# First SwiGLU, last two down parts: the four sums of weight blocks made by accumulating transfers, in two more raw buffers

## The chip, the cores and the metric

The kernel runs on one core of a Trainium2 chip. The metric is the device time of one execution in microseconds (us). A core has TensorE (PE, matrix products), VectorE (DVE), ScalarE (ACT), GpSimd (POOL) and SyncE (SP), which run their own rows of instructions in order and wait for each other by semaphores. Transfers between HBM and the on-chip memory are issued by SP, ACT or POOL and carried out by 16 DMA engines that all issuers share. A transfer issued by POOL can add what it reads to what lies at its destination (an accumulating transfer).

## The reference

Two layers of a decoder, sequence 512, width 1024, all in float32. Each layer is SwiGLU, a mixer with two kinds of attention, and a second SwiGLU:

```python
D_MODEL, SEQ, DEPTH, D_FF = 1024, 512, 2, 2816

def _swiglu(h, w_gate_up, w_down):
    g, u = jnp.split(h @ w_gate_up, 2, axis=-1)
    return (jax.nn.silu(g) * u) @ w_down

for layer in range(DEPTH):
    x = x + 0.5 * _swiglu(_rmsnorm(x, ffn1_norm[layer]), ffn1_w_gate_up[layer], ffn1_w_down[layer])
    x = x + _hybrid_mixer(_rmsnorm(x, mix_norm[layer]), w_in[layer], ...)
    x = x + 0.5 * _swiglu(_rmsnorm(x, ffn2_norm[layer]), ffn2_w_gate_up[layer], ffn2_w_down[layer])
return _rmsnorm(x, final_norm)
```

The change touches `@ w_down` of the first SwiGLU of layer 0 alone.

## The kernel before

**Products.** Float32 precision comes from splitting each operand into a high and a low half (`split`: ScalarE casts the value to the high half, line 86, VectorE subtracts to get the low half, line 87) and taking three matmuls of the halves (`mm3`, lines 421 to 423). A large product is cut into 2 x 2 blocks and made by seven block products instead of eight (a Strassen-Winograd scheme). On the weight side these need four sums of the blocks 11, 12, 21, 22. The seven products are named by digits and run in the order `STEADY = "1562734"`. Their weight operands are: 1: block 11; 2: block 12; 4: block 22; 5: 21 + 22; 7: 11 + 21; 6: 11 + 21 + 22; 3: 12 + 11 + 21 + 22.

**Parts.** A SwiGLU's inner width 2816 is cut into six parts (counted from 0). For each part there is a gate-up stage ("u") and a down stage ("d"); the order is u0, u1, d0, u2, d1, ... u5, d4, d5. The next part's turned hidden block (`turn_h`: transposes on TensorE, copies on ScalarE, differences on VectorE, lines 523 to 530) is made while the down stage before it runs. Each product of a down stage is 12 matmuls, followed by two updates of x on VectorE (line 552).

**Weights.** `forms` makes the weight operand of each product, in order. `get` loads a block (or a sum) into a raw buffer, 128 x 1024 floats (512 KB): `raw_tile` issues plain loads on SP (line 104); the sums for 5 and 7 get the second block by an accumulating transfer that POOL issues (line 137). The sum for 6 is made on VectorE by adding 5's sum to block 11 in place (line 148), and that for 3 by adding this result to block 12 (line 152). `make` splits the raw operand into one of five ring tiles (`wg`). Raw buffers have fixed names: down parts 4 and 5 of the first SwiGLU use s2 (11), R2 (7), V0 (22), V3 (12) and s0 (5); the gate-up part u5 before them uses among others s1 and V2. A raw buffer is given to its next user when the products in `last` are made.

**Order.** The program is written in the order of the products, with each weight made four products ahead (`next_w(ahead=4)`) and loads asked for up to 6 or 9 products ahead (the first number of each unit). A scheduler then fixes the row of each engine, and waits are added between the rows. Rows run in order: what waits on an engine holds up all that stands behind it there.

Of the kernel before, what the change touches and what calls it, by code (L numbers as in the profile page):

```python
# [12 lines left out]
ALU = mybir.AluOpType  # L13
# [42 lines left out]
def trunk(ctx, tc, xT, x, gains, gain_row, w_gu, w_dn, w_in, w_ff, w_out, fbias, lams, subln, consts, rope, out):  # L56
    nc = tc.nc
    act, dve, pool, pe, sp = nc.scalar, nc.vector, nc.gpsimd, nc.tensor, nc.sync
# [16 lines left out]
    def home(tag, shape, dt, name):  # L75
        return sb.tile(shape, dt, tag=tag, name=name, bufs=1)
# [13 lines left out]
    def split_w(src, hi, lo):  # L90
        w = min(step[0], src.shape[-1])
        for o in range(0, src.shape[-1], w):
            split(src[:, o:o + w], hi[:, o:o + w], lo[:, o:o + w])
        return hi, lo

    def ring_tile(tag, cols):
        g = home(tag, [P, 2, 1024], F32R, "wg")
        return g[:, 0, :cols], g[:, 1, :cols]

    def raw_tile(tag, cols, src):  # L100
        t = home(tag, [P, 1024], F32, "raw")
        w = min(step[0], cols)
        for o in range(0, cols, w):
            sp.dma_start(out=t[:, o:o + w], in_=src[:, o:o + w])
        return t[:, :cols]
# [6 lines left out]

    busy = set()

    def forms(order, groups, cols, where):

        raw = {}
        keys = [(f, h) for f in order for h in range(groups)]
        if order == FIRST:

            keys[:2 * groups] = [(f, h) for h in range(groups) for f in order[:2]]
        seen = set()

        last = {"11": ("2", "6"), "12": ("3",), "22": ("4",), "5": ("5", "6"), "7": ("7",)}

        def get(b, h, must=True):
            if (b, h) in raw:
                return raw[b, h]
            tag = where(b, h)[0]
            if tag in busy:  # L130
                assert not must, (tag, b, h)
                return None
            busy.add(tag)
            if b in "57":
                one, two = {"5": ("21", "22"), "7": ("11", "21")}[b]
                t = raw_tile(tag, cols, where(one, h)[1])
                pool.dma_start(out=t, in_=where(two, h)[1], accum_op=ALU.add)  # L137
            else:
                t = raw_tile(tag, cols, where(b, h)[1])
            raw[b, h] = t  # L140
            return t
        uses = {"1": "11", "2": "12", "5": "5", "6": "5", "3": "12", "7": "7", "4": "22"}

        def make(f, h, tag):
            src = get(uses[f], h)
            if f == "6":
                src = get("11", h)
                dve.tensor_tensor(out=src, in0=get("5", h), in1=src, op=ALU.add)
            w = split_w(src, *ring_tile(tag, cols))
            seen.add((f, h))  # L150
            if f in "26" and ("2", h) in seen and ("6", h) in seen:
                dve.tensor_tensor(out=raw["12", h], in0=raw["12", h], in1=raw["11", h], op=ALU.add)
            for b, fs in last.items():
                if f in fs and all((g, h) in seen for g in fs):
                    busy.discard(where(b, h)[0])
            return w
        return [(9 if f in "57" else 6, lambda f=f, h=h: get(uses[f], h, False),
                 lambda tag, f=f, h=h: make(f, h, tag)) for f, h in keys]

    def push(units, i):  # L160
# [6 lines left out]
    def gu_units(n, c, order):  # L167
        groups = PARTS_OF[n][c] // 256
        base = sum(8 if w == 512 else 4 for w in PARTS_OF[n][:c])
        tags = {("11", 0): "R0", ("11", 1): "R1", ("7", 0): "R2", ("22", 0): "V0", ("7", 1): "V1",  # L170
                ("22", 1): "V2", ("12", 0): "V3", ("12", 1): "V4", ("5", 0): "s0", ("5", 1): "s1"}
        if groups == 1:

            tags = {(b, 0): tags[b, 1] for b in ("11", "7", "22", "12", "5")}
        return forms(order, groups, 1024, lambda b, h: (
            tags.get((b, h)), w_gu[n, base + BLOCKS.index(b) * groups + h] if b in BLOCKS else None))

    def dn_units(n, c, order, second=False):
        cols = PARTS_OF[n][c] // 256 * 512
        base = sum(PARTS_OF[n][:c]) // 256 * 4 * 512  # L180
        tags = {"11": "s2", "7": "R2", "22": "V0", "12": "V3", "5": "s0"}
        if second:

            tags = {"11": "R1", "7": "V1", "22": "V4", "12": "V2", "5": "s1"}
            if n % 2 == 0:
                tags.update({"7": "R0", "22": "R0"})

        def where(b, h):
            src = None
            if b in BLOCKS:  # L190
                o = base + BLOCKS.index(b) * cols
                src = w_dn[n, o * P:(o + cols) * P].rearrange("(p s) -> p s", p=P)
            return tags.get(b), src
        return forms(order, 1, cols, where)

    def plain(src, raw_tag, tag):
        got = []
# [15 lines left out]
    NCH = len(PARTS_OF[0])  # L213
# [12 lines left out]
    def pair_units(n):  # L226
        own = {s: iter(dn_units(n, NCH - 2 + i, "".join(u[0] for u in PAIR if u[1] == s), i == 1))
               for i, s in enumerate("ab")}
        return [next(own[u[1]]) for u in PAIR]
# [7 lines left out]
    for n in range(2 * DEPTH):  # L237
        l = n // 2
        if n % 2 == 1:
            for i in range(24 + len(OUT_K)):  # L240
                k = OUT_K[i - 24] if i >= 24 else None
                tag = MIX[i % 3] if i < 24 else None if k >= 4 else MIX[(i - 28) % 3]
                stream.append(plain(w_in[l, i] if i < 24 else w_out[l, k], f"R{(i + 1) % 3}", tag))
        r = 0
        for kind, c in parts_of(n):
            if (n, kind, c) != (0, "u", 0):
                r = push(pair_units(n) if kind == "dd" else
                         (gu_units if kind == "u" else dn_units)(n, c, part_order(kind, c)), r)
# [1136 lines left out]
    for l in range(DEPTH):  # L1385
        n = 3 * l + 1
# [112 lines left out]
```

## Time and profile before

| | |
|---|---|
| time, median of 3 runs | 1848.77 us (1848.69 to 1849.81) |
| the profiled execution's own time | 1847.17 us |
| its span, first to last instruction | 1845.4 us |
| TensorE busy, share of the span | 1822.7 us, 99% |
| VectorE busy | 1587.1 us, 86% |
| ScalarE busy | 1138.2 us, 62% |
| POOL busy | 133.2 us, 7% |
| mean granted TensorE clock | 0.997 |
| moved by DMA | 301.81 MB, mean 164 GB/s |
| L148 and L152, 128 x 1024 additions on VectorE | 63 each, 1.22 us each |

In a row of a timeline the first number is the start in us from the span's beginning, the second how long the rows merged into it took; then engine, line, operation, out<-in, and in brackets the idle time of the engine before it and what ended it. `SPq` is SP's queue. A table by stretches gives, for each, its length and the busy time of each engine with its count of instructions, then the granted clock of TensorE, the busy share of the DMA engines and GB/s. "DMA to landing" is the time from the issue of a transfer to the semaphore that tells of its end.

### The profile page before, as it was taken

How to read it: one execution, taken by the hardware profiler on the slowest of the kernel's cores; microseconds unless marked ns; L12 is line 12 of the kernel's file. 1: busy time of each engine (PE TensorE's matmuls, PEld its weight loads, DVE VectorE, ACT ScalarE, POOL GpSimd, SP SyncE). 2: the span in 40 equal slices, each digit the busy share in tenths (PEclk: the TensorE clock that was granted, in tenths of full speed). 3: DMA queues.
4: the chain of work that ended last, by engine and by line, in shares of the span. 5: the costliest groups of instructions: out<-in, count | busy, mean ns of one | idle time of the engine just before them, and what ended most of it. 6: DMA issues, size and time to landing. Idle time of an engine off the chain costs nothing.

```text
span 1845.4 us, 24412 instructions
## 1 busy us (share of the span) xinstructions
PE 1822.7 (99%) x8638; PEld 1495.5 (81%) x8638; DVE 1587.1 (86%) x2488; ACT 1138.2 (62%) x1816; POOL 133.2 (7%) x161
## 2 busy tenths in 40 slices
PE   9999999999999999999999999999999999999997
PEld 5888888778878888888878888897788788888886
DVE  7898899878686998899998898997787869898897
ACT  7555555657795755554676554555677957455555
POOL 2010000000000100000000000100000000000001
PEclk9999999999999999999999999999999999999999
DMA  9786655244336766667667767723333467776661
GB/s 315 205 232 182 186 148 158 80 126 110 95 106 174 213 194 177 186 174 200 157 177 205 194 157 205 203 76 118 110 110 101 127 167 194 205 201 177 168 168 58
DMA packets 94603, 301.81 MB, mean 164 GB/s; under 512 B 12616, under 2 KB 15176, under 8 KB 94480
## 3 DMA queue, kind: packets, MB, share of 16 engines
q1 hardware_dynamic: 73888, 230.15, 37.6%
q0 software_dynamic: 19296, 68.17, 21.3%
q10 hardware_dynamic: 1296, 1.93, 0.3%
q8 instruction: 68, 1.11, 0.2%
q14 instruction: 55, 0.45, 0.1%
HBM read 283.33 MB, written 2.20 MB: 155 GB/s over the span
## 4 chain that ended last, share of the span: by engine, by line
PE 85%; DVE 6%; ACT 5%; DMA 2%; issue 1%; SPq 0%; DVEq 0%; ACTq 0%; POOL 0%; POOLq 0%
PE ps_c L423 12%; PE ps_c L422 12%; PE ps_c L421 12%; PE ps L421 9%; PE ps L422 9%; PE ps L423 9%; PE ps_a L421 3%; PE ps_a L422 3%; PE ps_a L423 3%; PE ps_t L523 2%; PE ps_g L1318 2%; DVE wg L87 1%; ACT pg L927 1%; ACT pg L929 1%; PE ps_b L939 1%
## 5 line engine op out<-in xcount | busy, mean ns | idle before, releaser
L86 ACT CAST wg<-raw 128x1024 fp32r<-128x1024 f32 (+1 forms) x525 | 540.0, 1032 | 496.8 <-PE ps_c L423 199.4
L87 DVE TENSOR_TENSOR wg<-raw,wg 128x1024 fp32r<-128x1024 f32 (+1 forms) x525 | 622.1, 1192 | 107.3 <-ACT wg L86 106.0
L421 PE MATMUL ps_c<-wg,xf 128*128 128x512 f32 (+1 forms) x736 | 277.6, 377 | 1.4 <-ACT wg L86 1.4
L422 PE MATMUL ps_c<-wg,xf 128*128 128x512 f32 (+1 forms) x736 | 276.3, 375 | 0.0
L423 PE MATMUL ps_c<-wg,xf 128*128 128x512 f32 (+1 forms) x736 | 275.8, 375 | 0.0
L421 PE MATMUL ps<-wg,xf 128*128 128x512 f32 (+1 forms) x552 | 210.7, 382 | 0.7 <-ACT xf L86 0.5
L422 PE MATMUL ps<-wg,xf 128*128 128x512 f32 (+1 forms) x552 | 207.4, 376 | 0.1
L423 PE MATMUL ps<-wg,xf 128*128 128x512 f32 (+1 forms) x552 | 206.8, 376 | 0.0
L421 PEld LDWEIGHTS ps_c<-wg,xf 128*128 128x128 f32 x736 | 138.4, 188 | 28.0 <-ACT wg L86 1.8
L422 PEld LDWEIGHTS ps_c<-wg,xf 128*128 128x128 f32 x736 | 138.6, 188 | 25.3 <-DVE wg L87 0.3
L423 PEld LDWEIGHTS ps_c<-wg,xf 128*128 128x128 f32 x736 | 138.5, 188 | 25.0
L421 PE MATMUL ps_c<-wg,hf 128*128 128x512 f32 x352 | 137.8, 391 | 1.5 <-DVE x L552 1.4
L137 POOL DMA_DIRECT2D raw<-w_gu x86 | 74.6, 868 | 891.6 <-DMA raw<-w_gu 418.3
L422 PE MATMUL ps_c<-wg,hf 128*128 128x512 f32 x352 | 137.1, 390 | 0.0
L423 PE MATMUL ps_c<-wg,hf 128*128 128x512 f32 x352 | 137.0, 389 | 0.0
L421 PEld LDWEIGHTS ps<-wg,xf 128*128 128x128 f32 x552 | 103.9, 188 | 19.3 <-ACT xf L86 1.3
L423 PEld LDWEIGHTS ps<-wg,xf 128*128 128x128 f32 x552 | 103.8, 188 | 18.9
L422 PEld LDWEIGHTS ps<-wg,xf 128*128 128x128 f32 x552 | 104.0, 188 | 17.9 <-DVE wg L87 0.5
L552 DVE SCALAR_TENSOR_TENSOR x<-ps_c,x 128x512 f32<-128x512 f32 x168 | 108.9, 681 | 1.3 <-PE ps_c L423 0.9
L421 PE MATMUL ps_a<-XA,wg 128*128 128x512 f32 x256 | 104.2, 408 | 1.2 <-ACT XA L375 1.1
L421 PE MATMUL ps<-wg,hf 128*128 128x512 f32 x264 | 103.2, 391 | 0.0
L422 PE MATMUL ps<-wg,hf 128*128 128x512 f32 x264 | 102.9, 390 | 0.0
(292 smaller groups left out, 3519.6 us busy)
## 6 DMA issues: line engine op xcount, KB each, us to landing
raw<-w_gu SPq DMA_DIRECT2D x218, 512.0 KB
raw<-w_dn SPq DMA_DIRECT2D x100, 512.0 KB
raw<-w_gu POOLq DMA_DIRECT2D x86, 512.0 KB, 6.9
raw<-w_in SPq DMA_DIRECT2D x48, 512.0 KB
raw<-w_dn POOLq DMA_DIRECT2D x40, 512.0 KB, 6.4
kdup<-qk_t SPq DMA_DIRECT2D x64, 128.0 KB
raw<-w_out SPq DMA_DIRECT2D x16, 512.0 KB
raw<-w_dn SPq DMA_DIRECT2D x20, 256.0 KB
```

The costliest lines, as they stand in the source:

```text
L86: act.copy(out=hi, in_=src)
L87: dve.tensor_tensor(out=lo, in0=src, in1=rf(hi), op=ALU.subtract)
L137: pool.dma_start(out=t, in_=where(two, h)[1], accum_op=ALU.add)
L421: pe.matmul(p, lh, rh, start=start, stop=False, skip_group_check=again)
L422: pe.matmul(p, lh, rl, start=False, stop=False, skip_group_check=again)
L423: pe.matmul(p, ll, rh, start=False, stop=stop, skip_group_check=again)
L523: pe.transpose(pj[j][:, e * 256 + p * P:e * 256 + (p + 1) * P], hs[j][p][:, o:o + P], ident)
L552: dve.scalar_tensor_tensor(out=xc, in0=src, scalar=scale, in1=xc, op0=ALU.mult, op1=ALU.add)
L927: act.activation(out=e, in_=e, func=AF.Exp, scale=-1.0, bias=st[:, 0:1], accum_out=st[:, 2:3])
L929: act.mul(out=e, in_=e, mul=st[:, 4:5])
L939: pe.transpose(p[:, (qb - kb) * P:(qb - kb + 1) * P], probs[u][qb][:, kb * P:(kb + 1) * P], ident)
L1318: pe.matmul(pg[2 * half + j], gained(kp, e, half)[:, j * P:(j + 1) * P], w0[kp][:, e * S:(e + 1) * S], start=kp + e == 0, stop=kp == KP - ...
```

## The change

For down parts 4 and 5 of the first SwiGLU (`n == 0 and c >= NCH - 2`) all four sums are made by transfers: the first block is loaded plainly, and each further block is added by an accumulating transfer. Each addition to a buffer waits for the landing of the one before. Products 6 and 3 get raw buffers of their own, s1 and V2, which u5 used before. Their blocks are loaded again for it: for each part 2 more plain loads and 5 more accumulating transfers of 512 KB, and no addition on VectorE. Each raw buffer now belongs to one product and is given on when that product's split is made; units 5, 7, 6 and 3 may be asked for 9 products ahead. All other parts are made as before.

```diff
-    def forms(order, groups, cols, where):
+    def forms(order, groups, cols, where, by_dma=False):
...
         last = {"11": ("2", "6"), "12": ("3",), "22": ("4",), "5": ("5", "6"), "7": ("7",)}
+        chains = {"5": ("21", "22"), "7": ("11", "21"), "6s": ("11", "21", "22"), "3s": ("12", "11", "21", "22")}
+        if by_dma:
+            last = {"11": "1", "12": "2", "22": "4", "5": "5", "7": "7", "6s": "6", "3s": "3"}
...
-            if b in "57":
-                one, two = {"5": ("21", "22"), "7": ("11", "21")}[b]
-                t = raw_tile(tag, cols, where(one, h)[1])
-                pool.dma_start(out=t, in_=where(two, h)[1], accum_op=ALU.add)
+            if b in chains:
+                t = raw_tile(tag, cols, where(chains[b][0], h)[1])
+                for more in chains[b][1:]:
+                    pool.dma_start(out=t, in_=where(more, h)[1], accum_op=ALU.add)
...
         uses = {"1": "11", "2": "12", "5": "5", "6": "5", "3": "12", "7": "7", "4": "22"}
+        if by_dma:
+            uses.update({"6": "6s", "3": "3s"})
...
-            if f == "6":
+            if f == "6" and not by_dma:
                 src = get("11", h)
                 dve.tensor_tensor(out=src, in0=get("5", h), in1=src, op=ALU.add)
...
-            if f in "26" and ("2", h) in seen and ("6", h) in seen:
+            if not by_dma and f in "26" and ("2", h) in seen and ("6", h) in seen:
                 dve.tensor_tensor(out=raw["12", h], in0=raw["12", h], in1=raw["11", h], op=ALU.add)
...
-        return [(9 if f in "57" else 6, lambda f=f, h=h: get(uses[f], h, False),
+        return [(9 if f in ("57", "5763")[by_dma] else 6, lambda f=f, h=h: get(uses[f], h, False),
...
-        tags = {"11": "s2", "7": "R2", "22": "V0", "12": "V3", "5": "s0"}
+        tags = {"11": "s2", "7": "R2", "22": "V0", "12": "V3", "5": "s0", "6s": "s1", "3s": "V2"}
...
-        return forms(order, 1, cols, where)
+        return forms(order, 1, cols, where, n == 0 and c >= NCH - 2)
```

What stands in the rows of two engines now. First POOL, from the sum for product 5 of part 4 to the mixer's mask `tri`. Before, raw_2164 is 5's sum and raw_2244 that of 7 in part 4, raw_2375 and raw_2415 the same two in part 5; the names in brackets are the semaphores waited for (DMAHW: a transfer issued by SP or ACT, DMASW: one issued by POOL):

```order
L137 DMA raw_2164<-w_dn 128x1024 [waits DMAHW5_49,DMASW2_49,DVE_49]
L137 DMA raw_2244<-w_dn 128x1024 [waits DMAHW7_49,DMASW3_49,DVE_49]
L137 DMA raw_2375<-w_dn 128x1024 [waits DMAHW3_49,DMASW4_49,DVE_49]
L675 CAST tri_2808<-tri_f_2619 128x512 [waits DMAHW5_49,PE_49]
L137 DMA raw_2415<-w_dn 128x1024 [waits DMASW7_49,DMAHW7_49,DMASW5_49,DVE_49]
```

Now, in part 4: raw_2164 is 5's sum, raw_2208 that of 6 (in s1), raw_2248 that of 7, raw_2323 that of 3 (in V2). In part 5: raw_2364 (5), raw_2388 (6), raw_2428 (7), raw_2450 (3):

```order
L140 DMA raw_2164<-w_dn 128x1024 [waits DMAHW5_49,DMASW2_49,DVE_49]
L140 DMA raw_2208<-w_dn 128x1024 [waits DMASW7_49,DMAHW6_49,DVE_49,Activation_49]
L140 DMA raw_2208<-w_dn 128x1024 [waits DMASW5_49]
L140 DMA raw_2248<-w_dn 128x1024 [waits DMAHW0_49,DMASW3_49,DVE_49]
L140 DMA raw_2323<-w_dn 128x1024 [waits DMAHW7_49,DMAHW4_49,DVE_49]
L140 DMA raw_2323<-w_dn 128x1024 [waits DMASW1_49,DMASW0_49]
L140 DMA raw_2364<-w_dn 128x1024 [waits DMAHW6_49,DMASW4_49,DVE_49]
L140 DMA raw_2323<-w_dn 128x1024 [waits DMASW1_49]
L140 DMA raw_2388<-w_dn 128x1024 [waits DMAHW0_49,DMASW6_49,DVE_49]
L140 DMA raw_2388<-w_dn 128x1024 [waits DMASW4_49]
L140 DMA raw_2428<-w_dn 128x1024 [waits DMAHW3_49,DMASW7_49,DVE_49]
L140 DMA raw_2450<-w_dn 128x1024 [waits DMAHW4_49,DMASW3_49,DVE_49]
```

Ten issues are new; the second and third addition to a buffer wait only for the one before it (DMASW). The mask's cast now stands behind all of them.

Second ScalarE, in part 4, from product 2's cast to the copies of the first transposes of `turn_h`. Before, raw_2283 is block 12 (the first time as it is, the second time with L152's addition in it, product 3), raw_2244 is 7's sum, raw_2336 block 22 (product 4), `hb` and `ws` are the copies:

```order
L86 CAST wg_2390<-raw_2283 128x1024 [waits DMAHW1_49,PE_49,Activation_49]
L627 DMA tri_f_2619<-consts 128x512 [waits DMAHW5_49]
L86 CAST wg_2412<-raw_2244 128x1024 [waits DMASW5_49,PE_49,Activation_49]
L86 CAST wg_2434<-raw_2283 128x1024 [waits DVE_49,PE_49,Activation_49]
L86 CAST wg_2479<-raw_2336 128x1024 [waits DMAHW2_49,PE_49,Activation_49]
L526 COPY hb_2463<-ps_t_2453 128x512 [waits PE_49]
L528 COPY ws_2465<-ps_t_2454 128x256 [waits PE_49]
```

Now raw_2287 is block 12, raw_2248 7's sum, raw_2323 3's sum and raw_2345 block 22:

```order
L86 CAST wg_2404<-raw_2287 128x1024 [waits DMAHW2_49,PE_49,Activation_49]
L632 DMA tri_f_2633<-consts 128x512 [waits DMAHW1_49]
L86 CAST wg_2423<-raw_2248 128x1024 [waits DMASW7_49,PE_49,Activation_49]
L86 CAST wg_2447<-raw_2323 128x1024 [waits DMASW3_49,PE_49,Activation_49]
L86 CAST wg_2495<-raw_2345 128x1024 [waits DMAHW3_49,PE_49,Activation_49]
L531 COPY hb_2479<-ps_t_2469 128x512 [waits PE_49]
L533 COPY ws_2481<-ps_t_2470 128x256 [waits PE_49]
```

The order is the same; the cast for product 3 waited for VectorE before, and now waits for a transfer that POOL issues (DMASW3, the third addition to raw_2323).

## The prediction

> **What bounds the kernel now.** First the busy times on the page and the shares of its chain of waits (span 1845.4 us):
>
> ```profile
> PE 1822.7 (99%) x8638; PEld 1495.5 (81%) x8638; DVE 1587.1 (86%) x2488; ACT 1138.2 (62%) x1816; POOL 133.2 (7%) x161
> PE 85%; DVE 6%; ACT 5%; DMA 2%; issue 1%; SPq 0%; DVEq 0%; ACTq 0%; POOL 0%; POOLq 0%
> ```
>
> TensorE is busy nearly always, so an edit gains only where TensorE stands still, and any stall of TensorE is paid in full. Next, busy time by stretch around the two parts that change. Their products run from 299.6 to about 344 us; the mixer's first work follows.
>
> ```profile
> core 0: us, PE busy (x) PEld busy (x) DVE busy (x) ACT busy (x) POOL busy (x), PEclk, DMA share, GB/s
> 299.60:309.40 9.80, 9.80 (x52) 8.28 (x51) 9.80 (x15) 5.58 (x8) 1.67 (x2) 1.00 0.83 215
> 309.40:319.20 9.80, 9.80 (x45) 7.74 (x43) 8.75 (x15) 6.12 (x10) 0.30 (x1) 1.00 0.53 127
> 319.20:331.00 11.80, 10.34 (x44) 7.75 (x43) 11.80 (x16) 5.26 (x5) 0.00 (x0) 1.00 0.00 0
> 331.00:344.00 13.00, 12.97 (x64) 10.38 (x64) 12.22 (x18) 7.22 (x16) 0.00 (x0) 1.00 0.31 99
> ```
> ```profile
> 340.00:345.00 5.00, 3.97 (x22) 2.84 (x20) 4.57 (x9) 3.42 (x8) 0.00 (x0) 1.00 0.66 214
> 345.00:350.00 5.00, 4.30 (x21) 2.91 (x22) 4.75 (x12) 4.85 (x14) 0.00 (x0) 1.00 0.31 104
> ```
>
> VectorE has no idle time in the third row, and TensorE loses 11.80 - 10.34 = 1.5 us behind it. That is all that a lighter VectorE can win inside the two parts; 1.03 + 0.70 = 1.7 us more are lost at the mixer's start (340 to 350). The DMA engines are busy 0.83 of the time in the first row: this is when part 4's last sums must arrive under the change.
>
> **What is removed.** Four additions on VectorE: L148 and L152, once for each part. The timeline of VectorE:
>
> ```profile
> 262.19 1.22 DVE L148 TENSOR_TENSOR raw<-raw 128x1024 f32<-128x1024 f32 x1
> ...
> 287.31 1.23 DVE L87 TENSOR_TENSOR wg<-raw,wg 128x1024 fp32r<-128x1024 f32 x1 [1.49 <-ACT wg L86]
> ...
> 291.29 1.23 DVE L148 TENSOR_TENSOR raw<-raw 128x1024 f32<-128x1024 f32 x1
> ...
> 300.88 1.22 DVE L152 TENSOR_TENSOR raw<-raw 128x1024 f32<-128x1024 f32 x1
> ...
> 307.11 0.42 DVE L529 TENSOR_TENSOR ws<-hb,ps_t 128x256 f32<-128x256 f32 x1
> ...
> 322.06 1.21 DVE L148 TENSOR_TENSOR raw<-raw 128x1024 f32<-128x1024 f32 x1
> 323.20 1.28 DVE L552 SCALAR_TENSOR_TENSOR x<-ps,x 128x512 f32<-128x512 f32 x2
> ...
> 327.27 1.21 DVE L152 TENSOR_TENSOR raw<-raw 128x1024 f32<-128x1024 f32 x1
> ```
>
> That is 4 x 1.22 = 4.9 us of VectorE. The two at 291.29 and 300.88 lie where TensorE loses nothing (9.80 of 9.80), so they win nothing. The two of part 5 stand ahead of TensorE's 1.5 us stall and would remove it: -1.5 us.
>
> **What is added.** For each part two plain loads on SP (four issues in all; nothing waits for SP's sequencer) and five accumulating transfers on POOL. POOL is 7% busy, so ten issues cost nothing as work; the cast of `tri` that now stands behind them is first used at 434.6, some 95 us after they end:
>
> ```profile
> L791 PEld LDWEIGHTS ps_a<-tri,sh x16: 87/88/88, 434.6 to 1348.1; 128*8 128x8 f32 x16
> ```
>
> What costs is that the transfers of one sum are a chain: each waits until the one before has landed. The longest is product 3's sum in part 4: one plain load, then three additions into V2. V2 comes free with the split at 287.31, so the load is issued at 287.31 + 1.23 = 288.5. How long a link takes, from the queues' timelines:
>
> ```profile
> 276.80 0.33 SPq L104 DMA_DIRECT2D raw<-w_dn  x1
> ```
> ```profile
> 262.27 0.86 POOL L137 DMA_DIRECT2D raw<-w_dn  x1 [11.54 <-DVE wg L87]
> 280.57 0.86 POOL L137 DMA_DIRECT2D raw<-w_dn  x1 [17.44 <-DVE wg L87]
> 297.79 0.88 POOL L137 DMA_DIRECT2D raw<-w_dn  x1 [16.36 <-DVE p L493]
> ```
>
> The load of 276.80 is followed by its addition at 280.57: 3.8 us. From issue to landing, three additions taken alone, those issued at 262.27, at 297.79 and, in a crowded stretch, at 162.78:
>
> ```profile
> DMA to landing us min/median/max: 5.5/5.5/5.5
> ```
> ```profile
> DMA to landing us min/median/max: 6.4/6.4/6.4
> ```
> ```profile
> DMA to landing us min/median/max: 8.5/8.5/8.5
> ```
>
> So the chain is: first addition issued at 288.5 + 3.8 = 292.3. It shares the engines with part 5's next loads, the rope table and `tri_f`, all issued between 291 and 298; I take 7.6, between 6.4 and 8.5. Then a restart of POOL, which no row shows between two chained additions; its bounds are 0 and the 0.86 of POOL's own instruction, and I take 0.6. Second addition: 6.5, like the row at 297.79, whose surroundings it shares. Third: 5.8, nearer the quiet row, since SP's next load waits for this very chain. Landing: 292.3 + 7.6 + 0.6 + 6.5 + 0.6 + 5.8 = 313.4. Bounds: 292.3 + 3 x 5.5 = 308.8, and 292.3 + 3 x 8.2 + 2 x 0.86 = 318.6. Product 6's chain has one link fewer and a buffer, s1, that comes free with the addition at 262.19: by the same arithmetic it ends at 263.4 + 5 + 2 x 6.5 + 0.6 = 282, twelve us ahead of its split, and is hidden; were it late, TensorE would lose as below.
>
> The Trainium skill speaks against such a wait. Its page "DMA: Bandwidth & Descriptors", section "Anatomy of one DMA — SWDGE (gpsimd) path", fits a transfer from POOL at about 2.0 us plus bytes over 436e3; for 512 KB that is an estimate of 3.2 us, and by it the chain would be ready by about 304. No addition of 512 KB in this trace is so short; the quiet one above took 5.5. I keep the rows.
>
> **Who waits for it.** ScalarE's timeline and TensorE's:
>
> ```profile
> 302.55 1.05 ACT L86 CAST wg<-raw 128x1024 fp32r<-128x1024 f32 x1 [1.66 <-PE ps_c L423]
> 305.27 1.05 ACT L86 CAST wg<-raw 128x1024 fp32r<-128x1024 f32 x1 [1.67 <-PE ps L423]
> 306.23 0.58 ACT L526 COPY hb<-ps_t 128x512 f32<-128x512 f32 x1
> ```
> ```profile
> 308.18 0.39 PE L422 MATMUL ps_c<-wg,hf 128*128 128x512 f32 x1
> 308.41 0.39 PE L423 MATMUL ps_c<-wg,hf 128*128 128x512 f32 x1
> 308.64 1.03 PE L523 MATMUL ps_t<-ident,p 128*128 128x128 f32 x8
> 309.43 0.48 PE L421 MATMUL ps<-wg,hf 128*128 128x512 f32 x1
> ```
>
> The cast of 302.55 is that of product 3's weights, the one of 305.27 product 4's. Now the first waits until 313.4, and everything behind it in ScalarE's row waits with it: product 4's cast, and then the copy of the first transposes (L526). TensorE's second transposes (308.64) write the bank that this copy empties, and TensorE runs its row in order, so products 2 and 7, whose weights lie ready, wait too. Casts of 1.0 and 1.0 and the copy's 0.5 bring the transposes to 313.4 + 2.5 = 315.9: a stall of 315.9 - 308.6 = 7.3 us.
>
> After it VectorE has its backlog. Its split of product 3 ends at 313.4 + 1.0 + 1.2 = 315.6; then come two updates (1.2), product 4's split (1.1) and two evictions (L529 and L530, 0.4 each), to 318.7, while TensorE has done the transposes (0.8) and the first half of product 2 (six matmuls, 0.23 apart) by 318.1. So it waits 0.6. Counted on with the same durations it waits twice more, 1.1 before product 7 and 1.2 before product 4: together +2.9.
>
> Part 5's own long chain is started by the late split, at 315.7, behind two additions of product 6 and one of product 7 on POOL; with links of 6 it lands at about 338.4, which is 25.0 after 313.4. TensorE, counted on, wants that sum 25.2 us after: it just arrives, cost 0, with 0 to 5 as its bounds. Behind part 5 the mixer's first transposes find VectorE less behind than before; of the 1.7 us lost there I take half back, -0.9 (bounds -1.7 and 0).
>
> A long stall has one more price. TensorE's granted clock, before and in the one stretch where it falls ahead of the second mixer half:
>
> ```profile
> 538.90:542.30 3.40, 2.53 (x12) 1.56 (x13) 2.51 (x8) 3.40 (x8) 0.00 (x0) 1.00 0.18 43
> 542.40:545.80 3.40, 3.40 (x12) 2.87 (x11) 2.65 (x8) 2.84 (x9) 0.00 (x0) 0.50 0.39 134
> ```
>
> After 3.4 us with 0.9 idle, TensorE ran 3.4 us at 0.50. A stall of 7 us should bring that too: 3.4 x 0.5 = 1.7 us, of which about half falls into the waits for VectorE just counted. I take +0.8, bounds 0 and 1.7. The Trainium skill ("TensorE: Matmul & The Clock Gate", Part 1) has the clock halved after an idle window of about 3.4 us; the trace agrees on the length, and with the page's rule charged in full the sum would be 0.9 more.
>
> **The sum.** -1.5 + 7.3 + 2.9 + 0 - 0.9 + 0.8 = +8.6 us. The profiled execution took 1847.17 us, 1.6 under the median of the runs, 1848.77, which is what is compared; there 8.6 us make 1857.4.
>
> **Rivals.** (1) *The chain lands in time*, by 308.6 - 2.5 = 306.1: links of (306.1 - 292.3) / 3 = 4.6, restart included. For it: the rows are of additions whose destination had long been loaded by another queue, none is of a chain, and a first addition's 5.5 may hold a start-up that the second has not. Against it: three links at the shortest row still end at 308.8, 2.7 us late. Then only the gains are left, -1.5 - 0.9: 1846.4. The Trainium skill's fit above, from "DMA: Bandwidth & Descriptors", would give this case. (2) *The chain is late by little.* Links of 5.5 with no restart land at 308.8, 4.6 us earlier than I take; the stall shrinks to 2.7, the clock stays up: about 1852.0. For it: the added loads leave SP quiet from 304 on. Against it: the DMA share of 0.83. (3) *Part 5's chain is late as well.* Its three additions start behind three others on POOL; at 8 us a link, it lands 5 us past TensorE's need, and product 3 of part 5 stalls as part 4's did: 1857.4 + 5 = 1862.4. For it: POOL's one row in order. Against it: by then most loads are done (share 0.00 between 319 and 331).
>
> **How the numbers follow.** Forecast 0.63 (1854 to 1860), rival 1 0.06, rival 2 0.16, rival 3 0.15. The point is the forecast's, 1857.4. Rival 2 and the low bound of the chain reach to 1851.5, rival 3 and the high bound (318.6) to 1863; this range leaves out rival 1 and the tails. Within 0.2% (3.7 us, about what a measurement of this kernel can tell from no change) are rival 1 mostly and the better part of rival 2: 0.13. Faster by more would need more stall than TensorE has here (1.5 and 1.7): 0.03. Slower: 0.84.
>
> **What would show it.** The profile after should have: on ScalarE, the cast of product 3 at about 313 instead of 302.55, its idle time ended by a DMA of `w_dn`; three POOL issues about 6 to 8 us apart from 292; TensorE idle for about 7 us from 308.6, and a stretch at 0.50 soon after; L148 and L152 at 61 instead of 63; the end of part 5 near 352; everything from 350 on shifted and unchanged. I am wrong if an addition into a buffer just loaded lands in about 4 us, if the accumulating transfers run side by side, or if ScalarE reaches the copy before the cast.

## The result and the profile after

The changed kernel takes 1862.89 us (median of 6 runs, 1858.70 to 1866.04) against 1847.95 (6 runs, 1845.75 to 1849.81): ratio 1.0079, 95% interval 1.0068 to 1.0089, or 14.9 us slower. The forecast was 8.6 us slower. The profiled execution is one of the longest, 1865.99 us, span 1864.2; the sums below are its own, and it took 18.8 us more than the 1847.17 of the execution profiled before.

The page after, busy times and the shares of the chain of waits:

```profile
PE 1827.3 (98%) x8638; PEld 1498.4 (80%) x8638; DVE 1582.9 (85%) x2484; ACT 1137.6 (61%) x1816; POOL 141.8 (8%) x171
PE 70%; ACT 5%; DVE 4%; DMA 2%; issue 1%; DVEq 0%; SPq 0%; ACTq 0%
```

VectorE has lost its four additions (2488 to 2484 instructions, 4.2 us) and POOL has its ten issues more. TensorE has the same 8638 matmuls and is busy 4.6 us longer: matmuls that ran at half clock. The rest of the time is idle. POOL's timeline first, where x2 merges two issues:

```profile
283.39 0.88 POOL L140 DMA_DIRECT2D raw<-w_dn  x1 [6.81 <-DMA raw<-w_dn]
294.07 0.86 POOL L140 DMA_DIRECT2D raw<-w_dn  x1 [9.80 <-issue]
303.82 1.76 POOL L140 DMA_DIRECT2D raw<-w_dn  x2 [8.88 <-DMA raw<-w_dn]
311.59 1.76 POOL L140 DMA_DIRECT2D raw<-w_dn  x2 [6.02 <-DMA raw<-w_dn]
...
334.86 0.86 POOL L140 DMA_DIRECT2D raw<-w_dn  x1 [10.58 <-DMA raw<-w_dn]
```

The issues of 294.07, 303.82 and 311.59 are the three additions to product 3's sum in part 4. From issue to landing they took, asked of each one by one:

```profile
DMA to landing us min/median/max: 9.4/9.4/9.4
...
DMA to landing us min/median/max: 7.3/7.3/7.3
...
DMA to landing us min/median/max: 5.5/5.5/5.5
```

So the sum landed at 311.59 + 5.5 = 317.1; the forecast was 313.4. POOL restarted 0.35 to 0.5 us after each landing.

Why the first link took 9.4 us can be followed in the queues of the DMA engines. `q0` is POOL's queue and `q1` SP's, which carries the plain loads; the numbers are packets, MB and the share of the 16 engines' time. The first row is the first 3.43 us after the issue of 294.07. The other two are the same stretch of the same link in the run with part 4 alone (below), where the link took 5.4 us:

```profile
q1 hardware_dynamic: 155, 0.57, 67.9%
...
q0 software_dynamic: 67, 0.27, 56.9%
q1 hardware_dynamic: 125, 0.45, 32.4%
```

Here no packet of the addition moved for 3.4 us, although the engines were only 0.68 busy; there half of it had moved. The engines' share over the whole link doesn't tell the two apart: 0.88 here, 0.94 there. The crowded row of the forecast (162.78, 8.5 us) began like the slow one, with 0.04 MB in as long a stretch. Why POOL's packets start so late in some runs isn't shown. The second link moved 0.03 MB in its first 3 us, beside 1.00 MB of plain loads.

ScalarE's timeline, the rows whose idle time a transfer ended, and the first copy behind:

```profile
317.15 1.99 ACT L86 CAST wg<-raw 128x1024 fp32r<-128x1024 f32 x2 [15.75 <-DMA raw<-w_dn]
319.05 0.58 ACT L531 COPY hb<-ps_t 128x512 f32<-128x512 f32 x1
...
334.70 0.25 ACT L677 CAST wfs<-lt 128x64 fp32r<-128x64 f32 x1 [5.51 <-DMA lt<-w_ff]
346.03 3.89 ACT L86 CAST wg<-raw 128x1024 fp32r<-128x1024 f32 x4 [8.02 <-DMA raw<-w_dn]
```

The first row is product 3's cast of part 4 (302.55 before) with product 4's merged into it, the last that of part 5. The third waits for `w_ff`, a load for the mixer. TensorE's timeline, all waits of over half a microsecond up to the mixer, and the last matmul ahead of the first:

```profile
308.92 0.39 PE L428 MATMUL ps_c<-wg,hf 128*128 128x512 f32 x1
319.68 1.97 PE L528 MATMUL ps_t<-ident,p 128*128 128x128 f32 x8 [10.37 <-ACT hb L531]
...
333.91 0.50 PE L426 MATMUL ps_c<-wg,hf 128*128 128x512 f32 x1 [0.83 <-DVE x L557]
...
342.48 0.50 PE L426 MATMUL ps_c<-wg,hf 128*128 128x512 f32 x1 [0.79 <-DVE x L557]
...
349.08 0.47 PE L426 MATMUL ps<-wg,hf 128*128 128x512 f32 x1 [2.46 <-ACT wg L86]
...
351.32 0.79 PE L426 MATMUL ps_c<-wg,hf 128*128 128x512 f32 x1 [0.75 <-DVE x L557]
...
364.97 0.50 PE L426 MATMUL ps_a<-XA,wg 128*128 128x512 f32 x1 [0.95 <-ACT XA L380]
```

Before, TensorE's waits between 309 and 347 were these; the row of 346.99 is the mixer's first product, that of 364.97 after:

```profile
330.96 0.47 PE L421 MATMUL ps_c<-wg,hf 128*128 128x512 f32 x1 [1.35 <-DVE x L552]
345.06 0.44 PE L359 MATMUL ps_t<-ident,x 128*128 128x128 f32 x2 [1.09 <-DVE x L552]
345.66 0.87 PE L359 MATMUL ps_t<-ident,x 128*128 128x128 f32 x6 [0.16 <-DVE x L552]
346.99 0.51 PE L421 MATMUL ps_a<-XA,wg 128*128 128x512 f32 x1 [0.46 <-ACT XA L375]
```

Last, stretches after, cut where the granted clock changes:

```profile
309.10:312.70 3.60, 0.21 (x1) 0.00 (x0) 0.00 (x0) 0.00 (x0) 1.11 (x2) 1.00 0.90 171
312.70:322.90 10.20, 3.22 (x12) 2.94 (x13) 4.67 (x8) 4.02 (x7) 2.44 (x3) 0.50 0.84 167
322.90:350.20 27.30, 23.22 (x99) 17.75 (x97) 21.73 (x32) 12.44 (x16) 3.21 (x4) 1.00 0.66 137
350.20:357.10 6.90, 6.15 (x17) 4.51 (x16) 4.94 (x8) 2.42 (x7) 0.00 (x0) 0.51 0.00 0
```

There are two stretches at half clock. The first begins inside the stall, 3.4 us after its start, and ends 3.2 us after it. In it TensorE works 3.22 us, which costs half of it, 1.6; in the second 6.15, which costs 3.1.

The sum at the mixer's first product: 364.97 - 346.99 = 18.0, of which 0.5 is a wait for a weight at 9.55, long ahead of the change. New waits 10.37 + 0.83 + 0.79 + 2.46 + 0.75 = 15.2; half clock 1.6 + 3.1 = 4.7; gone are 1.35 in part 5 and 1.71 - 0.95 = 0.8 at the mixer's start. 15.2 + 4.7 - 2.1 = 17.8, against 17.5 measured. The 0.8 between 18.0 and 18.8 comes later and was not followed.

### The profile page after: what moved, and what is told of

It reads as the page before. It is cut to its first block, busy times and chain, and to the rows that moved or that the text cites. A ratio compares the mean times of both kernels' runs of the same rounds, so it can differ in the third digit from the quotient of the medians.

```text
span 1864.2 us, 24448 instructions
## 1 busy us (share of the span) xinstructions
PE 1827.3 (98%) x8638; PEld 1498.4 (80%) x8638; DVE 1582.9 (85%) x2484; ACT 1137.6 (61%) x1816; POOL 141.8 (8%) x171
## 3 DMA queue, kind: packets, MB, share of 16 engines
q8 instruction: 68, 1.11, 0.2%
## 4 chain that ended last, share of the span: by engine, by line
PE 70%; ACT 5%; DVE 4%; DMA 2%; issue 1%; DVEq 0%; SPq 0%; ACTq 0%
PE ps_c L428 10%; PE ps_c L427 10%; PE ps_c L426 10%; PE ps L426 7%; PE ps L427 7%; PE ps L428 7%; PE ps_a L426 3%; PE ps_a L427 3%; PE ps_a L428 3%; PE ps_t L528 2%; DVE wg L87 1%; ACT pg L932 1%; ACT pg L934 1%; PE ps_a L720 1%; PE ps_a L718 1%
```

## The experiments

All times are medians beside runs of the kernel before on the same chip; the first four ran beside a median of 1847.08, the next four beside 1847.72, the last three timed ones beside 1847.49.

| run | median, us | against before, 95% interval |
|---|---|---|
| 3's sums earlier, other buffer | 1856.15 | 1.0034 to 1.0059 |
| part 4 alone | 1856.71 | 1.0038 to 1.0063 |
| part 5 alone | 1849.99 | 1.0008 to 1.0026 |
| no addition for 3 | 1842.18 | 0.9960 to 0.9982 |
| two additions for 3 | 1850.92 | 1.0006 to 1.0023 |
| overwriting transfers for 3 | 1854.98 | 1.0021 to 1.0046 |
| only 6 by transfers | 1848.76 | 1.0001 to 1.0020 |
| sums from on-chip buffers | 1842.88 | 0.9963 to 0.9986 |
| no addition at all | 1843.40 | 0.9968 to 0.9986 |
| all transfers, unread | 1849.17 | 1.0000 to 1.0018 |
| on-chip, in place | 1855.01 | 1.0029 to 1.0054 |

**Product 3's sums earlier.**

```diff
-        tags = {..., "6s": "s1", "3s": "V2"}
+        tags = {..., "6s": "s1", "3s": "R0" if (n, c) == (0, NCH - 2) else "V2"}
```

> Product 3's sum of part 4 goes into R0 (free once u5's product 6 is split, about 20 us before V2), that of part 5 into V2; all transfers and their number stay as in the changed kernel. Theory A (the sum of product 3 lands too late, 317.05 against the 306 that ScalarE needs, and everything behind its cast waits): the three additions start near 277 and end before 300, the 10.4 us stall of TensorE and both stretches at clock 0.50 go, and with VectorE 4.9 us lighter the time is 1845 to 1848. Theory B (14 more transfers of 512 KB crowd the DMA engines, so that loads land late whatever buffer they go to): the time stays within 4 us of 1862.9, and ScalarE's idle times name other loads of w_dn.

1856.15: neither theory. ScalarE's and TensorE's timelines (of an execution of 1852.18, the shortest of its five):

```profile
302.52 1.05 ACT L86 CAST wg<-raw 128x1024 fp32r<-128x1024 f32 x1 [1.82 <-DMA raw<-w_dn]
318.07 1.05 ACT L86 CAST wg<-raw 128x1024 fp32r<-128x1024 f32 x1 [5.05 <-DMA raw<-w_dn]
329.27 2.00 ACT L86 CAST wg<-raw 128x1024 fp32r<-128x1024 f32 x2 [9.28 <-DMA raw<-w_dn]
```
```profile
321.50 0.50 PE L426 MATMUL ps_c<-wg,hf 128*128 128x512 f32 x1 [2.46 <-DVE x L557]
```

Product 3's cast of part 4 is back at 302.52 and the stall of 10.4 is gone, as theory A has it; but the sum landed only at 302.4, and now the sums for 5 and 6 of part 5 are the late ones (318.07 and 329.27). POOL's row is a queue: a chain moved up in it moves the others back. An earlier buffer for one sum doesn't cure the lateness; it moves it to other sums in that queue.

**Each part alone.**

```diff
-        return forms(order, 1, cols, where, n == 0 and c >= NCH - 2)
+        return forms(order, 1, cols, where, n == 0 and c == NCH - 2)
```

> The change in part 4 alone; part 5 adds on VectorE as before. Theory A: the stall of 10.4 us and the half-clock stretch behind it stay, about 12 us; part 5 has no late chain (2.5 us less) and perhaps no second half-clock stretch at 350 (3.4 us less), but its VectorE waits of 1.5 us come back, grown by the backlog: 1858 to 1862. Theory B: half of the added transfers, half of the loss: about 1855.

The same with `c == NCH - 1`:

> The change in part 5 alone; part 4 adds on VectorE as before. Theory A: V2 is free from 288.5 and product 3 of part 5 is needed some 25 us later than that of part 4, so three links of 5.5 to 9.4 us from 294 end by 322, in time; TensorE loses nothing and wins the 1.5 us in front of which the two additions stood, and part of the 1.7 at the mixer's start: 1845 to 1848. Theory B: half of the added transfers, half of the loss: about 1855.

Part 4 alone costs 9.6 us, 1.3 short of theory A's range and 1.7 over theory B's number. Its trace has the stall (7.14 us here, the links 5.4, 6.9 and 7.3) and one half-clock stretch of 6.8 us. Part 5 alone costs 2.9 where A promised a gain, and the trace of the shortest execution, 1845.53, doesn't show them. Another execution was traced:

> The kernel with the change in part 5 alone once more, for its trace: the first trace is of an execution of 1845.5 us, the shortest of 11 (median 1850.0), and shows one wait of 2.04 us. If the rest of the 3 us lies in crowding, a trace near 1850 shows the load of w_ff (or the sum for product 5) landing later than there, TensorE waiting 3 us or more for VectorE near 321, and a stretch at clock 0.50 of 3.4 or 6.8 us behind it; if product 3's or 6's sum of part 5 is late after all, ScalarE's cast there has an idle time ended by a DMA of w_dn.

It took 1851.26 (before, beside it: 1845.56). ScalarE and TensorE in it:

```profile
322.15 0.24 ACT L677 CAST wfs<-lt 128x64 fp32r<-128x64 f32 x1 [7.68 <-DMA lt<-w_ff]
...
324.78 0.80 PE L426 MATMUL ps_c<-wg,hf 128*128 128x512 f32 x1 [5.05 <-DVE x L557]
```

and in the execution of 1845.53:

```profile
318.70 0.24 ACT L677 CAST wfs<-lt 128x64 fp32r<-128x64 f32 x1 [4.65 <-DMA lt<-w_ff]
...
321.33 0.50 PE L426 MATMUL ps_c<-wg,hf 128*128 128x512 f32 x1 [2.04 <-DVE x L557]
```

No sum is late; late is `w_ff`, issued at 311.97 and 311.55; before the change it was issued at 311.52 and ready by 316.64. Its cast stands in ScalarE's row ahead of the next cast of `hf`, VectorE waits for that, and TensorE for VectorE. In the longer execution a half-clock stretch of 3.4 us follows. While `w_ff` was under way, POOL's queue moved 1.01 MB in the longer execution and 0.55 in the shorter, against 0.39 before the change. That fits crowding of the engines, and it varies from execution to execution; no run takes the crowd away from `w_ff` alone.

**The number of links.**

```diff
-        "3s": ("12", "11", "21", "22")}
+        "3s": ("12",)}
```

> Product 3's operand in both parts is block 12 alone, loaded plainly; blocks 11, 21 and 22 are left out of it, so six accumulating transfers fall away and product 6 keeps its own two-link chain. Theory A: no late landing, time 1845 to 1848; TensorE idles no 10 us near 309 and has no half-clock stretch at 312 or 350. Theory B (crowding, 8 of 14 added transfers left): about 1856. A third possibility, that product 6's chain also costs, would show as an idle time of ScalarE ended by a DMA ahead of product 6's cast, and a time above 1850.

and with `("12", "11", "21")`:

> Product 3's sum without block 22, which is left out of it in both parts: two additions instead of three. Late-sum theory: the sum of part 4 lands near 311 (where the second link of the changed kernel landed) instead of 317.05, so the stall of TensorE at 309 shrinks from 10.4 to about 4.5 us, the half-clock stretch behind it to 3.4 us or none, and part 5's cast of product 3 no longer waits: 1850 to 1855. If instead the number of bytes decides, two of 14 added transfers fewer: about 1861.

1842.18, 1850.92 and, with all three, 1862.89. Each against the kernel before beside it: with no link 4.9 us faster, with two 3.2 slower, with three 14.9 slower. So two links cost 8.1 us and the third 11.7 more. The time with two lies in the expected range, but not by the expected stall: the sum of part 4 landed at 307.1 instead of 311 (links of 5.4 and 7.8), and the stall at 309 is 0.2. What remains are waits of 0.4 to 0.9 for VectorE and one of 1.11 for product 3's cast in part 5, 4.0 in all in an execution of 1848.86. So the third link is the dearest: after two, the cast stands 4.6 us later than before and TensorE hardly stalls; the third is paid in full, with half clock on top. With product 6's two links still there, the run without additions for 3 loses nothing: ScalarE waits 2.29 for them in part 5, TensorE doesn't.

**Adding or overwriting.**

```diff
-                    pool.dma_start(out=t, in_=where(more, h)[1], accum_op=ALU.add)
+                    pool.dma_start(out=t, in_=where(more, h)[1], **({} if b == "3s" else {"accum_op": ALU.add}))
```

> Product 3's three further transfers overwrite instead of adding, so that its operand is block 22 alone (12, 11 and 21 are left out of it); bytes read, issuer, order and waits are as in the changed kernel. If the adding itself is what makes a link long (a packet's read and write at the destination), the links of part 4 shrink from 9.4, 7.3 and 5.5 us to 3.5 to 5 us, the sum lands by 308 and the time is 1844 to 1850. If the shared engines and POOL's issue make it long, the links stay within 1 us of those and the time stays at 1858 to 1866.

1854.98, between the two. The operand of part 4 landed at 312.7, 10 us after the cast's time before, and TensorE stalled for 6.33. The links of part 4 took 7.2, 5.8 and 5.6 us; in part 5, with little beside them, from issue to landing:

```profile
DMA to landing us min/median/max: 3.5/3.5/3.5
...
DMA to landing us min/median/max: 3.8/3.8/3.8
```

In the changed kernel the last two additions of part 5 took 5.4 and 5.3 (share of the engines 0.58 and 0.72, with the additions' own; 0.45 and 0.41 for the overwriting ones). So adding costs about 1.5 to 1.9 us a link by itself; what else the 9.4 and 7.3 hold goes in part with the late start of their packets, seen above, and is otherwise not settled. The Trainium skill's fit in "DMA: Bandwidth & Descriptors" ("Anatomy of one DMA — SWDGE (gpsimd) path"), an estimate of 3.2 us for 512 KB, is near the overwriting transfers and 2.1 us short for adding ones.

**Only product 6's sum by transfers.** Product 3's is 6's sum added to block 12 on VectorE:

```diff
...
+                dve.tensor_tensor(out=raw["12", h], in0=raw["12", h], in1=raw["6s" if by_dma else "11", h], op=ALU.add)
```

> Only the sum for product 6 is made by transfers; that for product 3 is made on VectorE again, by adding the sum for 6 to block 12 (one addition of 1.22 us in each part), without V2. Late-sum theory: two links in s1 end by 281 in part 4, and in part 5 nothing stands ahead of them but 5's and 7's sums; no cast waits for them: 1843 to 1848. If product 6's chain in part 5 is late (its split is wanted near 322), ScalarE has an idle time ended by a DMA there and the time is 1850 to 1853.

1848.76, 0.8 above the range of the first theory: one addition a part saved, and again `w_ff` late (ScalarE waits 4.64 for it, until 318.58, TensorE 2.02 behind it). No cast of product 6 waits long (1.34 in part 5). The trace is of an execution of 1847.00; four of the eleven took 1852.1 to 1853.4, and none of those was traced.

**Sums from buffers that are on the chip already.**

```diff
-            last = {"11": "1", "12": "2", "22": "4", "5": "5", "7": "7", "6s": "6", "3s": "3"}
+            last = {"11": "1", "12": "2", "22": "4", "5": ("5", "6"), "7": "7", "6s": ("6", "3"), "3s": "3"}
...
-                for more in chains[b][1:]:
-                    pool.dma_start(out=t, in_=where(more, h)[1], accum_op=ALU.add)
+                if b in ("6s", "3s"):
+                    pool.dma_start(out=t, in_=get({"6s": "5", "3s": "6s"}[b], h), accum_op=ALU.add)
+                else:
+                    pool.dma_start(out=t, in_=where(chains[b][1], h)[1], accum_op=ALU.add)
```

> All four sums by adding transfers, but with one link each: 6's sum adds 5's finished buffer to block 11, and 3's sum adds 6's finished buffer to block 12, by transfers from one on-chip buffer to another instead of two and three reads from HBM; VectorE adds nothing. 8 accumulating transfers for both parts instead of 14. Late-sum theory: 3's sum of part 4 is one link after 293, 299 to 303, in time; part 5 has four additions in POOL's row instead of seven and is in time too: 1841 to 1845, as without any link for product 3 (1842.2). If an on-chip source makes the link much longer than 10 us, product 3 is late again and the time is above 1850.

1842.88, 4.8 us faster than the kernel before (ratio 0.9974): this version beats both. Product 6's sum is block 11 plus 5's finished buffer, product 3's block 12 plus 6's; each is one link. Product 3's link in part 4 took 8.1 us, issued at 293.00, and landed at 301.1, in time. Stretches of it, and TensorE's only wait of over a quarter of a microsecond between 299 and 345:

```profile
299.50:309.30 9.80, 9.80 (x53) 8.32 (x52) 9.21 (x15) 5.85 (x9) 0.86 (x1) 1.00 0.95 275
309.30:321.00 11.70, 11.70 (x53) 9.66 (x52) 11.70 (x19) 6.70 (x11) 2.62 (x3) 1.00 0.97 243
321.00:340.00 19.00, 19.00 (x92) 15.76 (x91) 18.12 (x26) 10.84 (x19) 0.62 (x1) 1.00 0.29 88
```
```profile
342.75 0.50 PE L428 MATMUL ps_a<-XA,wg 128*128 128x512 f32 x1 [0.90 <-ACT XA L382]
```

The DMA engines are as full as in the changed kernel (0.95, 0.97), and TensorE doesn't stand still in these stretches: product 3's one link ends in time, and `w_ff`'s cast waits 0.38 us here.

**The additions and the transfers apart.** First the kernel before without its four additions, and nothing in their place:

```diff
...
-                dve.tensor_tensor(out=src, in0=get("5", h), in1=src, op=ALU.add)
+                if not last_two:
+                    dve.tensor_tensor(out=src, in0=get("5", h), in1=src, op=ALU.add)
...
-            if f in "26" and ("2", h) in seen and ("6", h) in seen:
+            if not last_two and f in "26" and ("2", h) in seen and ("6", h) in seen:
...
```

> The kernel before without its four additions on VectorE in the two parts and with no transfer in their place; products 6 and 3 use blocks 11 and 12 as they are, so the other blocks are left out of them. It measures what the removal alone is worth. By the forecast's two terms (1.5 in part 5 and 0.9 at the mixer's start) about 1845.3 against 1847.7; if the removal also takes the many waits under half a microsecond that stand between VectorE's updates and TensorE, 1842 to 1844, as the runs without links for product 3 (1842.2) and with on-chip sums (1842.9).

1843.40: the removal is worth 4.1 us, not 2.4. Then all 14 transfers, with the products fed by VectorE as before (its four additions are back):

```diff
...
-            uses.update({"6": "6s", "3": "3s"})
...
+        def want(f, h):
+            if by_dma and f in "63":
+                get(f + "s", h, False)
+            get(uses[f], h, False)
...
```

> All 14 accumulating transfers of the changed kernel run, into s1 and V2 too, but products 6 and 3 take their sums from VectorE as before, and nobody reads s1 and V2. If the late sums for product 3 (and in part 5 for 6) are the cost, no cast waits for them, the 10.4 us stall is gone and what is left is crowding (w_ff's load and the sums for 5 and 7 of part 5, which stand behind the chains on POOL): 1848 to 1854. If the bytes and POOL's row alone are the cost, 1858 or more.

1849.17: 1.7 us slower than before (interval from 0.0 to 3.3). So the bytes and POOL's row cost about 1.7 while nobody waits for the new sums. By subtraction, if the two costs add up, the other 13.2 of the 14.9 come with the waiting for them, and that although the additions are gone.

**On-chip, without the two buffers.**

```diff
...
+            if last_two and f == "1":
+                pool.dma_start(out=src, in_=get("5", h), accum_op=ALU.add)
+            if last_two and f == "2":
+                pool.dma_start(out=src, in_=raw["11", h], accum_op=ALU.add)
...
```

> On-chip adding transfers as in the run with 1842.9, but without the two more buffers: 5's finished sum is added into block 11's own buffer once product 1 is split, and the result into block 12's once product 2 is split, in the places of VectorE's two additions. Each link then has only two products (some 5.5 us) between the split that frees the buffer and the cast that needs the sum, against links of 4.6 to 8.1 us there. If the head start that the extra buffers give is what makes the on-chip sums free, ScalarE now waits up to 3 us for each of the four: 1850 to 1858. If a link into a buffer at rest takes 5 us and the slack behind ScalarE's casts (3 to 4 us) covers it: 1843 to 1846.

1855.01, the time of the first case, but with one long wait instead of four short ones. 6's sum in part 4 took 4.5 us, the shortest addition in these runs, and kept nobody waiting. That of product 3 is issued only at 302.36, behind another addition in POOL's row:

```profile
311.24 1.99 ACT L86 CAST wg<-raw 128x1024 fp32r<-128x1024 f32 x2 [10.62 <-DMA raw<-raw]
```

TensorE loses 5.24 us behind it. So, in these two orders of POOL's row, the two more buffers of the change were its good part; its three links more in each part (seven, against four in the version of 1842.88) were the bad one.

## Why the prediction was right or wrong

The sign, and the mechanism of the largest term, were right: product 3's sum of part 4 lands too late, ScalarE's row stops at its cast, the copy that empties the transposes' bank stands behind it, and TensorE stalls from 309 on. The signs promised for it are there (the cast at 317, the three issues, the idle time from 309, half clock), but for the end of part 5, near 363 instead of 352. The size was not: 8.6 forecast, 14.9 at the median, 17.5 in the profiled stretch. The time, 1862.89, lies just inside the stated range, whose upper end was 1863, and three of the six executions lie above it. That is luck: the end was drawn for a longer chain in part 4 or a late one in part 5, and the largest part of the excess in the profiled execution, half clock, was in neither. By its terms:

- **The stall, 7.3 forecast, 10.4 measured.** Late by the chain's links: 9.4, 7.3 and 5.5 against 7.6, 6.5 and 5.8, and 5.0 instead of 3.8 from load to first addition (289.08 to 294.07). The restart was smaller, 0.35 to 0.5 against 0.6. The step that failed is the price of the first two links. The rows it was taken from were not calmer by the engines' share (0.93 and 0.90, against 0.88 and 1.03 here); what tells the links apart is the late start, 3.4 us before the first packet of the first link moved. Of the rows only the crowded one had it, and the sum went half way between the rows. The landing stays within the bounds given (318.6). The first link is also what varies: 5.4 in the runs with part 4 alone and with two additions, 9.4 here.
- **Halved clock, 0.8 forecast, about 4.7 measured.** The worst-sized term, outside its bounds of 0 to 1.7. The first stretch, 10.2 us long instead of 3.4, lay mostly inside the stall and cost 1.6, within the bounds. What broke them is a second one of 6.9 us, 3.1, which followed part 5's wait; the forecast had that wait at nothing. That the sum charged one stretch and no more was its error.
- **Part 5's chain, 0 forecast, 2.5 measured.** It landed at 345.9, 28.8 us after part 4's instead of 25.0; its first addition, beside the sum for 7, took 11.1. Rival 3 had this mechanism, with its price at 5; its total, 1862.4, is near the measured time, but made up otherwise.
- **Backlog behind the stall, 2.9 forecast, 2.4 measured** (0.83, 0.79, 0.75): right in sum, and by luck. The three waits were to come within part 4, in product 2 and before 7 and 4; none did; TensorE was at half clock until 322.9. Only the 0.83 can be followed back to the stall: VectorE works without a pause from 318.2 until then. The 0.79 comes after VectorE had stood idle for 1.48 behind `w_ff`'s cast, the 0.75 behind part 5's wait.
- **The relief, 1.5 and 0.9 forecast.** In the changed kernel 1.35 and 0.8. Where nothing is late, the run without additions shows 4.1. The sum counted only the long waits; some short ones go too (0.35 between two matmuls at 321.6), but the whole difference is not accounted for. Mis-sized; the on-chip version collects all of it.
- **Product 6's chain, hidden: right** (its second addition, issued at 275.70, landed at 281.0; forecast 282). POOL's ten issues and `tri`: nothing, right.
- **`w_ff` was not in the working.** The longer execution with part 5 alone shows that its late landing can cost 5.05 us of TensorE.

Rivals 1 and 2 fell: around the two parts no adding link from HBM took less than 5.2 us in any run, and those of product 3's sum of part 4 took 5.5 to 9.4 in the changed kernel. What lies between the executions of one kernel (1858.7 to 1866.0) agrees with their mean clocks, 0.995 to 0.992, and with the first link's spread, but the shorter executions have no trace; so which of the two it is stays open.

## What to carry to other kernels

Where each transfer waits for the landing of the one before, price every link by rows from the same crowd, add them up, and leave room for a late start of any of them. The chain is free only if it ends before the engine that reads it gets there in its row; here two links nearly did and three did not. Look first for a partial sum that lies on the chip already: one link from it did what three from HBM could not, and gained 4.8 us. A small load for the next stage that shares the DMA engines, and whose reader stands ahead in an engine's row, belongs into the account too.

## What the runs showed of the hardware

Around the two parts an adding transfer of 512 KB from HBM, issued by POOL, took 5.2 to 5.5 us at its shortest, an overwriting one 3.5 to 3.8, an adding one from an on-chip buffer 4.5 to 5.2. At their longest, two of POOL's under way at a time among them, the same took 11.5, 10.5 and 8.8. Their length didn't follow the engines' share (5.4 us at 0.94, 9.4 at 0.88). It went, in part, with how soon POOL's packets began to move. Of the adding links from HBM with no other addition beside them, all that took 5.7 us or less had moved 0.16 MB or more after 3 us; those that had moved 0.05 or less took 7.4 to 9.4. Some with 0.16 to 0.18 still took 6.5 to 7.3.

Stretches at half clock were 3.4, 6.8 or 10.2 us long, steps of 3.4; the Trainium skill ("TensorE: Matmul & The Clock Gate", Part 1) gives a window of that length, and the trace agrees on it. What it takes to start one isn't settled. In the long stalls the clock fell during the stall, 3.4 us after its start in the changed kernel. A wait of 2.46 with 0.75 behind it was followed by 6.8 us, waits of 2.02 and 5.05 by 3.4, and waits of 1.35 and 2.04 by none. The rule that the forecast took from the same page of the Trainium skill, an idle window of about 3.4 us, doesn't cover the wait of 2.02, which is shorter.
